# Two neighbouring rows per partition for the gate and up weights of a mixture of experts

## The chip, the cores and the metric

The kernel runs on one core of one Trainium2 chip. The metric is device time in microseconds (us): from the start to the end of one execution, as the median of several runs. The profile shows one execution. Its engines are TensorE (PE for products, PEld for the weight loads into it), VectorE (DVE), ScalarE (ACT), GpSimd (POOL) and SyncE (SP), which mostly issues DMA transfers; sixteen DMA engines move the data between the memory of the chip and the core's SBUF.

## The reference

One layer of a diffusion backbone, for 256 latent and 256 context tokens of 2048 channels, all in float32. A modulated RMS norm feeds one input projection; a state-space branch and a gated short convolution follow, one output projection joins them, and a gated residual is added. Then comes the part that matters here: a second modulated norm, a router, and 16 experts that each choose their 32 best tokens.

```python
mod_lat = jnp.einsum('bd,de->be', jax.nn.silu(c), w_mod[layer]) + b_mod[layer]
sh1_l, sc1_l, g1_l, sh2_l, sc2_l, g2_l = jnp.split(mod_lat[:, None, :], N_MOD, axis=-1)
...
f_lat = modulate(rmsnorm(h_lat, norm_ffn_w[layer]), sh2_l, sc2_l)
aff = jax.nn.softmax(jnp.einsum('bnd,de->bne', h, w_router).astype(jnp.float32), axis=-1)
gates, idx = lax.top_k(jnp.swapaxes(aff, 1, 2), cap)
xe = jax.vmap(lambda hb, ib: hb[ib])(h, idx)
hid = jax.nn.silu(jnp.einsum('becd,edf->becf', xe, w_gate)) * jnp.einsum('becd,edf->becf', xe, w_up)
ye = jnp.einsum('becf,efd->becd', hid, w_down) * gates[..., None].astype(h.dtype)
```

`modulate(h, shift, scale)` is `h * (1 + scale) + shift`. For each expert w_gate and w_up are 2048 x 1024 and w_down is 1024 x 2048, so an expert's three matrices are 8 MiB each and all experts together 384 MiB. The sum over the channels `d` in the products with w_gate, w_up and w_router doesn't depend on the order in which the channels are taken, as long as both factors take them in the same order.

## The kernel before

Channels lie on the 128 partitions. A vector of 2048 channels is a tile of 128 partitions by 16 columns, and column k holds channels 128k to 128k+127; a matrix with 2048 rows is used in 16 tiles of 128 rows in the same way.

**Stages.** First the modulation for the input (`make_mods`, `mod_both`), in chunks of the channels, together with the first blocks of the input projection. Then the rest of the input projection (`gemm`, `gemm_part`), whose weights are loaded by `split_tile` on SP as `raw`, rounded on ScalarE (`whi`, line 89) and reduced to the remainder on VectorE (`wlo`, line 90); the state-space groups and the short convolution work on its results. The later modulation (shift sh2 and scale sc2 of the experts' input, gates g1 and g2) is spread between these blocks: `mod_lat` (lines 221 to 238) loads w_mod by GpSimd as `mraw` into two buffers, sums it on VectorE into `macc` (lines 230 and 232), and at the end of 512 columns transposes `macc` on TensorE (line 236) and reduces it (lines 237 and 238). There are 16 such chunks, four each for sh2, sc2, g1, g2. In the output projection they are loaded one row tile at a time (kn=1, 16 loads to a chunk), before that two at a time.

**Output projection and router.** `h`, the residual stream, lies with tokens on the partitions. As its columns are ready, it is transposed on TensorE (line 765), copied as `hT`, and multiplied with the router's weights `gwr`, which were loaded by SP (line 715) and scaled with G = (1 + sc2) * norm_ffn_w on VectorE (line 719). The top 32 tokens of each expert are found on VectorE; one-hot matrices `oh` follow.

**Experts.** A loop over the 16 experts (from line 877). Line 883 gathers an expert's tokens: 8 products of `oh` with 512 columns of `h` each, recorded as 16. Line 889 transposes them, and line 896 applies G and sh2, giving `xe` with channels on the partitions. Then, for each pair of row tiles k0, k0+1, line 914 loads one tile of w_gate and one of w_up, 1 MiB each, and line 920 multiplies `xe` with them:

```python
nc.sync.dma_start(t.rearrange("p (a b) -> p a b", a=2),
                  w[e_].rearrange("(k p) f -> p k f", p=P)[:, k0:k0 + 2, :])
```

Partition p so receives row 128 k0 + p and row 128 (k0+1) + p, two runs of 4 KB that lie 512 KB apart in memory. After the activation, line 940 loads w_down in 8 tiles of 128 rows, 1 MiB each, where partition p receives one row of 8 KB, and line 943 multiplies. The last expert's w_down is loaded column by column (line 961).

**What sets the order.** A scheduler places the instructions of each engine by their dependences and priorities; the kernel's text gives the priorities. Each engine, and each DMA queue, then takes its instructions in that order. Expert weights go through a ring of 8 KB slots (`wtile`): a slot is loaded again when the products that read it are done. The first slots become free during the output projection, so the first expert's weights are loaded ahead.

**Small parameters.** Before line 182 the rows of c, c_ctx, b_mod, the convolution and norm weights are loaded as r1, r2, r3 and transposed; `bcol` holds b_mod and `nffn` norm_ffn_w as columns. `late_cols` (line 181) does the same for a few that are needed later. GpSimd issues two of the loads (lines 120 and 101), then makes the index pattern `it` (line 125), from which `ident` is made on VectorE (line 127).

## Time and profile before

| what | us |
|---|---|
| three runs | 2017.79, 2019.6, 2024.4 |
| median | 2019.6 |
| span of the profiled execution, from the first to the last instruction | 2012.6 |

The page gives no time of its own for the profiled execution beyond that span; the median of the runs stands 7.0 us above it. Read the page in this order: the span and the chain that ended last (which engines and transfers set the end), then the busy time of the engines by stage, then the stage with the largest share of the chain, instruction by instruction. A busy share over 1 for DMA means that the times of neighbouring packets overlap a little. The profiled time has five parts: up to 20 us the start, to 870 us the input projection and its two branches, to 1010 us the output projection, to 1061 us its end and the router, and from there the experts.

### The profile page before, as it was taken

What the parts mean: (1) busy time and instruction counts of PE and PEld (TensorE: products, weight loads), DVE (VectorE), ACT (ScalarE), POOL (GpSimd) and SP (SyncE); (2) the same over time, 40 slices, a digit from 0 to 9 for tenths busy, and PEclk for the clock granted to TensorE, in tenths of its full rate; (3) what the DMA queues carried; (4) which work ended last, traced back from release to release, by engine and by line L of the source; (5) the groups of instructions that cost most, each with busy time, mean ns of one, the idle gap of its engine ahead of it and who ended that gap; (6) DMA issues with size and microseconds to landing.
All of it is one profiled execution on the core that took longest, in us unless ns stands there. A gap on an engine that the chain in (4) does not pass through costs nothing.

```text
span 2012.6 us, 25496 instructions
## 1 busy us (share of the span) xinstructions
PE 1663.9 (83%) x10316; PEld 995.4 (49%) x10316; DVE 906.1 (45%) x1389; ACT 516.4 (26%) x850; POOL 142.1 (7%) x207
## 2 busy tenths in 40 slices
PE   6999999899999999999988776667676677767675
PEld 4677997778798989777862111111111111111122
DVE  2448966778788878777642110111111111111113
ACT  4323656454566334343320000000000000000002
POOL 1001001111111221211200000000000000000000
PEclk9999999999999999999989889998889889898988
DMA  9975653646476989787888999999999999999997
GB/s 336 384 256 171 197 166 97 197 149 219 144 226 200 313 310 306 261 299 258 271 334 354 413 413 413 412 412 412 414 413 414 412 411 414 414 414 413 411 413 278
DMA packets 210774, 641.10 MB, mean 319 GB/s; under 512 B 17493, under 2 KB 50514, under 8 KB 194400
## 3 DMA queue, kind: packets, MB, share of 16 engines
q1 hardware_dynamic: 191248, 570.20, 74.8%
q0 software_dynamic: 19120, 68.22, 10.6%
q8 instruction: 81, 1.33, 0.3%
q10 hardware_dynamic: 288, 1.05, 0.1%
q14 instruction: 37, 0.30, 0.0%
HBM read 637.31 MB, written 2.10 MB: 318 GB/s over the span
## 4 chain that ended last, share of the span: by engine, by line
DMA 54%; PE 32%; DVE 7%; issue 4%; ACT 1%; SPq 1%; POOL 0%; DVEq 0%; ACTq 0%; POOLq 0%
DMA abig<-in_w_up_dram 12%; PE g L312 10%; DMA mraw<-in_w_mod_dram 10%; PE g L315 9%; DMA mwt<-in_w_up_dram 8%; DMA abig<-in_w_down_dram 8%; DMA mwt<-in_w_down_dram 6%; DMA ebig<-in_w_up_dram 6%; DMA raw<-in_w_in_dram 2%; DVE macc L232 2%; PE gu L920 2%; DVE wlo L90 2%; PE py L613 2%; PE g L747 1%; PE yd L943 1%
## 5 line engine op out<-in xcount | busy, mean ns | idle before, releaser
L315 PE MATMUL g<-abig,whi 128*128 128x256 f32 x2048 | 382.8, 289 | 16.2 <-DVE cvt L377 9.5
L89 ACT CAST whi<-raw 128x1024 fp32r<-128x1024 f32 x241 | 253.7, 1054 | 382.6 <-DMA raw<-in_w_in_dram 101.3
L90 DVE TENSOR_TENSOR wlo<-raw,whi 128x1024 fp32r<-128x1024 f32 x241 | 298.0, 1239 | 100.4 <-ACT whi L89 100.2
L315 PEld LDWEIGHTS g<-abig,whi 128*128 128x128 f32 x2048 | 325.3, 196 | 21.2 <-issue 15.5
L315 PE MATMUL g<-abig,wlo 128*128 128x256 f32 x1024 | 289.2, 289 | 2.0 <-DVE wlo L90 2.0
L920 PE MATMUL gu<-abig,xe 128*32 128x512 f32 x1088 | 205.6, 632 | 85.0 <-DMA abig<-in_w_up_dram 61.0
L232 DVE SCALAR_TENSOR_TENSOR macc<-mraw,csl,macc 128x512 f32<-128x512 f32 x240 | 187.0, 779 | 76.5 <-DMA mraw<-in_w_mod_dram 74.5
L925 DVE SCALAR_TENSOR_TENSOR hid<-hid,gu 64x512 f32<-64x512 f32 x16 | 10.9, 680 | 466.2 <-ACT hid L924 466.2
L312 PE MATMUL g<-abig,whi 128*128 128x512 f32 (+1 forms) x672 | 214.6, 398 | 2.7 <-ACT abig L296 2.5
L924 ACT ACTIVATE hid<-gu 64x512 f32<-64x512 f32 x16 | 9.5, 591 | 781.6 <-PE gu L920 781.6
L315 PEld LDWEIGHTS g<-abig,wlo 128*128 128x128 f32 x1024 | 197.6, 196 | 5.4 <-DVE wlo L90 3.4
L920 PE MATMUL gu<-mwt,xe 128*32 128x512 f32 x616 | 126.9, 660 | 52.0 <-DMA mwt<-in_w_up_dram 39.2
L747 PE MATMUL g<-whi,abig 128*128 128x512 f32 (+1 forms) x640 | 158.5, 351 | 1.9 <-ACT whi L89 1.6
L226 POOL DMA_DIRECT2D mraw<-in_w_mod_dram x152 | 101.3, 667 | 798.0 <-DVE macc L232 569.6
L920 PEld LDWEIGHTS gu<-abig,xe 128*32 128x32 f32 x1088 | 38.7, 111 | 238.0 <-DMA abig<-in_w_up_dram 108.6
L312 PEld LDWEIGHTS g<-abig,whi 128*128 128x128 f32 (+1 forms) x672 | 122.1, 185 | 44.2 <-issue 10.3
L312 PE MATMUL g<-abig,wlo 128*128 128x512 f32 (+1 forms) x336 | 130.5, 393 | 0.0
L747 PEld LDWEIGHTS g<-whi,abig 128*128 128x128 f32 x640 | 112.7, 191 | 17.7 <-ACT whi L89 2.0
L747 PE MATMUL g<-wlo,abig 128*128 128x512 f32 (+1 forms) x320 | 103.1, 354 | 9.1 <-DVE wlo L90 9.0
L954 DVE TENSOR_TENSOR ebig<-ebig,g 128x512 f32<-128x512 f32 x112 | 71.5, 684 | 80.0 <-PE g L950 80.0
L920 PE MATMUL gu<-ebig,xe 128*32 128x512 f32 x344 | 79.3, 699 | 30.1 <-DMA ebig<-in_w_up_dram 21.1
L943 PE MATMUL yd<-abig,hidT 128*32 128x512 f32 x512 | 71.6, 655 | 34.3 <-DMA abig<-in_w_down_dram 30.1
(311 smaller groups left out, 1561.6 us busy)
## 6 DMA issues: line engine op xcount, KB each, us to landing
raw<-in_w_in_dram SPq DMA_DIRECT2D x177, 512.0 KB, 4.6
abig<-in_w_up_dram SPq DMA_DIRECT2D x68, 1024.0 KB, 18.6
abig<-in_w_gate_dram SPq DMA_DIRECT2D x68, 1024.0 KB, 18.8
abig<-in_w_down_dram SPq DMA_DIRECT2D x64, 1024.0 KB, 20.0
mraw<-in_w_mod_dram POOLq DMA_DIRECT2D x104, 512.0 KB, 4.8
mwt<-in_w_down_dram SPq DMA_DIRECT2D x43, 1024.0 KB, 19.9
mwt<-in_w_gate_dram SPq DMA_DIRECT2D x39, 1024.0 KB, 20.0
mwt<-in_w_up_dram SPq DMA_DIRECT2D x38, 1024.0 KB, 18.6
```

The costliest lines, as they stand in the source:

```text
L89: nc.scalar.copy(hv, wv)
L90: nc.vector.tensor_tensor(lv, wv, hv.bitcast(F32), op=OP.subtract)
L226: nc.gpsimd.dma_start(w, w_mod.rearrange("(k p) c -> p k c", p=P)[:, k0:k0 + kn, c0:c0 + 512])
L232: nc.vector.scalar_tensor_tensor(acc, w[:, j], cs, acc, op0=OP.mult, op1=OP.add)
L312: nc.tensor.matmul(banks[ct][0:ncol], st, a[q][:, kk], start=beg, stop=end)
L315: nc.tensor.matmul(banks[ct // 2][0:ncol, o:o + L], st, a[q][:, kk, L:2 * L], start=beg and ct % 2 == 0, stop=end, skip_group_check=True)
L613: nc.tensor.matmul(oo, l, r, start=(i == 0), stop=(i == 3), skip_group_check=True)
L747: nc.tensor.matmul(ob[nn * t + m], yy[i][:, kk, P * t:P * t + P], w[:, j, n * m:n * m + n], start=(kt == order[0] and pi == 0), stop=(kt = ...
L920: nc.tensor.matmul(gu[32 * q:32 * q + 32], xe[:, k], wt[q // 2][:, 1024 * kk + 512 * (q % 2):1024 * kk + 512 * (q % 2) + 512], start=(k == ...
L925: nc.vector.scalar_tensor_tensor(hid, hid, 1.0, gu[0:64], op0=OP.add, op1=OP.mult)
L943: nc.tensor.matmul(yd[32 * q:32 * q + 32], hidT[:, j, 32 * c2:32 * c2 + 32], t[:, 512 * q:512 * q + 512], start=(kt == 0), stop=(kt == FF ...
L954: nc.vector.tensor_tensor(av, h[:, t, 512 * q:512 * q + 512] if e_ == 0 else av, pc[q], op=OP.add)
```

## The change

Two neighbouring rows of w_gate or w_up now go to one partition: partition p of pair b receives rows 256 b + 2p and 256 b + 2p + 1. One tile still holds the same 256 rows, 1 MiB. Row tile k = 2b + i therefore holds channels 256 b + 2p + i, and everything that meets these weights along the channels is paired in the same way:

- the gather of an expert's tokens and the transposes of `h` read every second column of `h`, first the even ones of 256, then the odd ones;
- sh2 and sc2 are transposed out of `macc` with a step of two (`paired`); g1 and g2 are not;
- norm_ffn_w and the parts of b_mod for sh2 and sc2 are loaded once more as `r4` (24 rows of 256, by GpSimd, at the very start), transposed with a step of two in `late_cols`, and kept as `pcol`;
- the router's weights are loaded in two transfers instead of one.

The products' and transposes' numbers and sizes stay. The diff also drops comments, which is left out here; line numbers shift by up to 20.

```diff
+    r4 = pp.tile([24, 256], F32, name="r4")
+    nc.gpsimd.dma_start(r4[0:8], norm_ffn_w[0].rearrange("(k p) -> k p", p=256))
+    nc.gpsimd.dma_start(r4[8:24], b_mod[0, 3 * D:5 * D].rearrange("(k p) -> k p", p=256))
...
+    pcol = const.tile([P, 3, KT], F32, name="pcol")
+    nffn = pcol[:, 0]
...
     def late_cols():
+        pt = sbank("pt")
+        for i in range(2):
+            nc.tensor.transpose(pt[:, 24 * i:24 * i + 24], r4.rearrange("p (c i) -> p i c", i=2)[:, i], ident[0:24, 0:24])
+        nc.vector.tensor_copy(pcol.rearrange("p a (b i) -> p i (a b)", i=2),
+                              pt[:, 0:48].rearrange("p (i c) -> p i c", i=2))
...
-    def mod_lat(c0, dst, pool, kn):
+    def mod_lat(c0, dst, pool, kn, bias, paired):
...
+            av = acc.rearrange("p (b c i) -> p b i c", b=2, i=2)
             for j in range(4):
-                nc.tensor.transpose(pc[:, P * j:P * j + P], acc[:, P * j:P * j + P], ident)
+                src = av[:, j // 2, j % 2] if paired else acc[:, P * j:P * j + P]
+                nc.tensor.transpose(pc[:, P * j:P * j + P], src, ident)
...
-            nc.vector.tensor_tensor(dst, dst, bcol[:, c0 // P:c0 // P + 4], op=OP.add)
+            nc.vector.tensor_tensor(dst, dst, bias, op=OP.add)
...
-            mod_lat((3, 4, 2, 5)[j] * D + 512 * q, dst, pool or mp, kn)
+            c0 = (3, 4, 2, 5)[j] * D + 512 * q
+            bias = pcol[:, 1 + j, 4 * q:4 * q + 4] if j < 2 else bcol[:, c0 // P:c0 // P + 4]
+            mod_lat(c0, dst, pool or mp, kn, bias, j < 2)
...
-    nc.sync.dma_start(wr, w_router.rearrange("(k p) e -> p k e", p=P))
+    for i in range(2):
+        nc.sync.dma_start(wr.rearrange("p (b i) e -> p i b e", i=2)[:, i],
+                          w_router.rearrange("(b p i) e -> p i b e", p=P, i=2)[:, i])
...
-                    nc.tensor.transpose(pt[:, o:o + P], h[:, t, P * (k + kk):P * (k + kk) + P], ident)
+                    hv = h[:, t, P * k:P * k + 2 * P].rearrange("p (c i) -> p i c", i=2)[:, kk]
+                    nc.tensor.transpose(pt[:, o:o + P], hv, ident)
...
+                    hv = h[:, t, 512 * q:512 * q + 512].rearrange("p (b c i) -> p b i c", b=2, i=2)
                     nc.tensor.matmul(pt[32 * q:32 * q + 32], oh[:, t, CAP * e_:CAP * e_ + CAP],
-                                     h[:, t, 512 * q:512 * q + 512], start=(t == 0), stop=(t == 1), skip_group_check=True)
+                                     hv, start=(t == 0), stop=(t == 1), skip_group_check=True)
...
-                                  w[e_].rearrange("(k p) f -> p k f", p=P)[:, k0:k0 + 2, :])
+                                  w[e_].rearrange("(b p i) f -> p b i f", p=P, i=2)[:, k0 // 2])
```

The change moves instructions too, since the scheduler places everything anew. Three places matter. The first is SP at the end of the first expert's loads; `mwt`, `ebig` and `abig` are the slots of the ring, and the sizes are those of the destination. Before:

```order
L914 DMA mwt<-in_w_up_dram 128x2x1024
L940 DMA mwt<-in_w_down_dram 128x2048 x5
L940 DMA ebig<-in_w_down_dram 128x2048 x3
L914 DMA abig<-in_w_gate_dram 128x2x1024
L914 DMA abig<-in_w_up_dram 128x2x1024
```

After:

```order
L934 DMA mwt<-in_w_up_dram 128x2048
L960 DMA mwt<-in_w_down_dram 128x2048 x5
L960 DMA ebig<-in_w_down_dram 128x2048 x3
L934 DMA abig<-in_w_gate_dram 128x2048
L934 DMA abig<-in_w_up_dram 128x2048
```

Nothing moved here; the loads of gate and up have the same form as those of w_down, one run per partition. From the router on, the order of SP is otherwise the same.

The second place is GpSimd at the start of the program (`r_70` is r1, `r_76` is r4). Before:

```order
L1019 UNCONDITIONAL_BRANCH
L120 DMA r_70<-in_ssm_conv_w_dram 72x128
L101 DMA r_70<-in_ssm_conv_b_dram 24x128
L125 ISA
L125 IOTA it 128x128
```

After:

```order
L1039 UNCONDITIONAL_BRANCH
L108 DMA r_76<-in_norm_ffn_w_dram 8x256
L109 DMA r_76<-in_b_mod_dram 16x256
L124 DMA r_70<-in_ssm_conv_w_dram 72x128
L101 DMA r_70<-in_ssm_conv_b_dram 24x128
L129 ISA
L129 IOTA it 128x128
```

Two loads now stand ahead of the index pattern.

The third place is VectorE at the start of the output projection, between the norms of the branches and the router's weights; `macc` is a step of the later modulation, here of its 14th chunk, whose first step reads `macc` from nothing. Before:

```order
L230 TENSOR_SCALAR macc_8145<-mraw_8146,csl_129 128x512
L636 TENSOR_TENSOR abig_8071<-ysc0_1717,abig_8070 128x1024
L636 TENSOR_TENSOR abig_8071<-ebig_5517,abig_8070 128x1024
L636 TENSOR_TENSOR abig_8077<-ebig_6359,abig_8076 128x1024
L232 SCALAR_TENSOR_TENSOR macc_8145<-mraw_8149,csl_129,macc_8145 128x512
L636 TENSOR_TENSOR abig_8077<-ebig_6359,abig_8076 128x1024
L90 TENSOR_TENSOR wlo_8662<-raw_8659,whi_8661 128x1024
L90 TENSOR_TENSOR wlo_8680<-raw_8677,whi_8679 128x1024
L719 TENSOR_TENSOR gwr_8117<-gwr_8117,mods_2482 128x16x16
L721 COPY srow_8138<-psb_8120 1x16
```

After:

```order
L242 TENSOR_SCALAR macc_8154<-mraw_8155,csl_132 128x512
L652 TENSOR_TENSOR abig_8079<-ysc0_1725,abig_8078 128x1024
L652 TENSOR_TENSOR abig_8079<-ebig_5525,abig_8078 128x1024
L652 TENSOR_TENSOR abig_8085<-ebig_6367,abig_8084 128x1024
L244 SCALAR_TENSOR_TENSOR macc_8154<-mraw_8158,csl_132,macc_8154 128x512
L652 TENSOR_TENSOR abig_8085<-ebig_6367,abig_8084 128x1024
L90 TENSOR_TENSOR wlo_8671<-raw_8668,whi_8670 128x1024
L244 SCALAR_TENSOR_TENSOR macc_8154<-mraw_8161,csl_132,macc_8154 128x512
L90 TENSOR_TENSOR wlo_8689<-raw_8686,whi_8688 128x1024
L737 TENSOR_TENSOR gwr_8125<-gwr_8125,mods_2490 128x16x16
L739 COPY srow_8147<-psb_8129 1x16
```

One more step of the modulation stands ahead of the router's weights, between the two remainders of w_out.

## Rows read from the trace of the kernel before

**Rows 1.** The page: span, all DMA packets, and the chain that ended last by engine.

```profile
span 2012.6 us, 25496 instructions
...
DMA packets 210774, 641.10 MB, mean 319 GB/s; under 512 B 17493, under 2 KB 50514, under 8 KB 194400
...
DMA 54%; PE 32%; DVE 7%; issue 4%; ACT 1%; SPq 1%; POOL 0%; DVEq 0%; ACTq 0%; POOLq 0%
```

**Rows 2.** By stage: stretch, length, busy us (instructions) by engine, granted clock, DMA share, GB/s.

```profile
20.00:330.00 310.00, 306.15 (x2103) 246.32 (x2099) 195.55 (x318) 140.80 (x222) 9.91 (x15) 1.00 0.71 233
330.00:870.00 540.00, 512.07 (x3392) 448.43 (x3391) 430.76 (x565) 263.52 (x445) 97.14 (x121) 0.98 0.70 230
870.00:1010.00 140.00, 130.24 (x704) 110.41 (x704) 100.02 (x131) 53.05 (x61) 25.36 (x48) 0.96 0.81 272
...
1061.00:1975.00 914.00, 644.42 (x3636) 141.75 (x3638) 133.97 (x242) 25.59 (x49) 0.58 (x1) 0.90 1.02 410
```

**Rows 3.** Timeline of TensorE, gate and up products: start us, length us, operation, idle before.

```profile
1882.94 1.05 PE L920 MATMUL gu<-mwt,xe 128*32 128x512 f32 x4 [0.65 <-DMA mwt<-in_w_gate_dram]
...
1911.07 1.91 PE L920 MATMUL gu<-abig,xe 128*32 128x512 f32 x12 [1.49 <-DMA abig<-in_w_up_dram]
```

**Rows 4.** The same view, products with w_down, in two experts.

```profile
1191.11 1.07 PE L943 MATMUL yd<-abig,hidT 128*32 128x512 f32 x8 [1.21 <-DMA abig<-in_w_down_dram]
...
1196.12 1.94 PE L943 MATMUL yd<-abig,hidT 128*32 128x512 f32 x8 [1.44 <-DMA abig<-in_w_down_dram]
...
1309.45 1.07 PE L943 MATMUL yd<-mwt,hidT 128*32 128x512 f32 x8 [1.20 <-DMA mwt<-in_w_down_dram]
...
1319.40 1.06 PE L943 MATMUL yd<-abig,hidT 128*32 128x512 f32 x8 [0.81 <-DMA abig<-in_w_down_dram]
```

**Rows 5.** Columns as in rows 2: gate and up alone, then w_down alone.

```profile
1140.00:1175.00 35.00, 26.14 (x124) 5.01 (x120) 4.51 (x8) 0.00 (x0) 0.00 (x0) 0.89 1.03 411
1177.00:1195.00 18.00, 12.29 (x88) 3.13 (x82) 2.80 (x6) 1.55 (x3) 0.00 (x0) 0.91 1.01 419
```

**Rows 6.** The same view around the first expert, and over the full stream.

```profile
1056.00:1066.00 10.00, 8.16 (x71) 3.11 (x75) 3.52 (x11) 0.59 (x1) 0.35 (x1) 1.00 0.36 125
1066.00:1076.00 10.00, 9.19 (x88) 2.60 (x80) 0.10 (x1) 0.59 (x1) 0.00 (x0) 1.00 1.01 416
...
1096.00:1960.00 864.00, 604.06 (x3338) 130.27 (x3332) 125.31 (x226) 24.04 (x46) 0.58 (x1) 0.90 1.02 413
```

**Rows 7.** The gather, then TensorE's transposes of h and macc: ns min/median/max.

```profile
1056.78 1.92 PE L883 MATMUL pt<-h,oh 128*32 128x512 f32 x16
...
L765 PEld LDWEIGHTS pt<-ident,h x32: 137/141/223, 1013.4 to 1037.9; 128*128 128x128 f32 x32
L765 PE MATMUL pt<-ident,h x32: 272/273/328, 1013.5 to 1038.0; 128*128 128x128 f32 x32
...
L236 PEld LDWEIGHTS pc<-ident,macc x64: 137/141/231, 338.7 to 1013.3; 128*128 128x128 f32 x64
```

**Rows 8.** Timeline of the program's first 20 us.

```profile
2.02 0.54 POOL L101 DMA_DIRECT2D r<-in_ssm_conv_b_dram  x1
2.64 0.28 POOL L125 IOTA it<- 128x128 f32 x1
...
3.99 0.31 PE L153 MATMUL pt<-ident,r 32*128 32x32 f32 x1 [3.99 <-DVE ident L127]
...
10.64 0.29 DVE L254 TENSOR_SCALAR diag<-ident,rs 128x128 f32<-128x128 f32 x1 [0.76 <-POOL rs L249]
```

**Rows 9.** The router's weights: their load, its landing, and the first products.

```profile
869.54 0.38 SPq L715 DMA_DIRECT2D gwr<-in_w_router_dram  x1
...
DMA to landing us min/median/max: 6.2/6.2/6.2
...
L718 PE MATMUL psb<-gwr,mods x32: 176/176/177, 883.3 to 884.1; 128*1 128x16 f32 x32
```

**Rows 10.** The later modulation's loads in the output projection: ns min/median/max, first and last start.

```profile
L226 POOL DMA_DIRECT2D mraw<-in_w_mod_dram x48: 536/538/592, 869.5 to 1008.8; - x48
```

More of the change, by code (lines that the diff above doesn't have):

```diff
@@ L174, in layer @@
     scw = col2[:, 0:48].rearrange("p (t k) -> p t k", t=3)
-    nmix, nffn, nssm, nsc = (col2[:, 48 + 16 * i:64 + 16 * i] for i in range(4))
+    nmix, _, nssm, nsc = (col2[:, 48 + 16 * i:64 + 16 * i] for i in range(4))
+    pcol = const.tile([P, 3, KT], F32, name="pcol")
+    nffn = pcol[:, 0]
     cw = col1[:, 0:72].rearrange("p (t k) -> p t k", t=3)
```

## The prediction

> **What bounds the kernel now.** I read the page's head and chain first, then the busy time by stage, then the stage that carries the chain. The span is 2012.6 us, and the chain that ended last is 54% DMA and 32% TensorE [rows 1]. The stage table splits that [rows 2]: from 20 to 870 us TensorE is busy 306.15 of 310 and 512.07 of 540 us, from 870 to 1010 us 130.24 of 140; this front is TensorE's. From 1061 to 1975 us it is busy only 644.42 of 914 us while the DMA share is 1.02. The experts wait for their weights.
>
> The rate inside that stage can be read without any packet rows, because TensorE starts on each transfer as it lands. With gate and up loads in flight its starts lie between 1882.94 and 1911.07 us, 12 starts and so 11 intervals: 28.13 / 11 = 2.557 us for each 1 MiB transfer [rows 3]. With w_down in flight four intervals run from 1309.45 to 1319.40 us (2.488 each) and two from 1191.11 to 1196.12 us (2.505 each) [rows 4]; I take the middle, 2.496 us. Both kinds move the same 1 MiB to the same 128 partitions. What differs is the piece: gate and up come in 4 KB runs, two to a partition, w_down in one 8 KB run. The windows that hold one kind alone agree: 411 GB/s for gate and up, 419 for w_down [rows 5]. The stream is not full before the first expert starts: at 1056 to 1066 us the share is 0.36, at 1066 to 1076 us it is 1.01, and it stays at 1.02 to 1960 us [rows 6]. It restarts when expert 0's products free slots.
>
> **Gate and up, the gain.** The order shows that each of these loads becomes 128x2048, the form in which w_down already stands; nothing is added to it. I therefore price it at w_down's 2.496 us: 2.557 - 2.496 = 0.061 us less for each. Expert 0's 16 loads are issued before the stream fills, and TensorE is busy 9.19 of the 10 us after 1066 us [rows 6] with products that don't wait for them, so they gain nothing at the end. Experts 1 to 15 have 15 x 16 = 240 loads in the full stream: 240 x 0.061 = 14.6 us. The bounds: 1 MiB at 411 and 419 GB/s is 2.551 and 2.503 us, 0.048 apart, 11.5 us; with the fastest w_down interval, 2.488, it is 0.069 and 16.6 us. I take 14.6, since the intervals count transfers and a window also holds its edges. TensorE does not become late: 604.06 us busy of 864 [rows 6], 70%. Next late is the same as now, the stream, then the last expert's column-wise w_down loads, which the change leaves alone.
>
> The same per piece: 1 MiB in half as many pieces lands 0.061 us sooner [rows 3, 4]; each of the 16 DMA engines has 128 / 16 = 8 pieces fewer per load, so the trace's price is 0.061 / 8 = 7.6 ns a piece. [...]
>
> **Token gather, residual transposes, modulation transposes.** The instruction counts stay; the operand read from SBUF now steps over every second float. In the 16 products that gather an expert's tokens it is the moving operand: 1.92 us in all for expert 0 [rows 7], on the path, because the experts' stream cannot restart before them; for the other 15 experts they lie beside the stream. In the 32 transposes of h it is the weight load, 141 ns median under products of 273 ns [rows 7], on the approach to the router, where TensorE is on the path. In 32 of the 64 transposes of the later modulation (the shift and scale of the experts' input) it is again the weight load, 141 ns [rows 7], in the front that TensorE bounds. No row shows such a step on TensorE. The lower bound is nothing, since as many elements are read; a gain is excluded, because nothing is left out. The upper bound is half rate: 1.92 + 32 x 0.141 + 32 x 0.141 = 10.9 us. The nearest rows, the same instructions on packed operands, say nothing of a step; I take 0, the price of the nearest rows, and leave 10.9 to a rival.
>
> [...]
>
> **Start.** Two loads of r4 stand ahead of the index pattern on GpSimd. A load there takes 0.54 us [rows 8], so the pattern, now at 2.64 us, comes about 1.1 us later, and so does ident, which is made from it and released the first product at 3.99 us. Who needs ident on the path is the diagonal at 10.64 us, and what it waited for last was the statistics of ctx from GpSimd [rows 8], not ident: over 6 us of cover. The transposes of c and b_mod at 3.99 us slide by the same 1.1 us, and their results are first needed after that diagonal. Cost 0; without the cover 1.1 us.
>
> **late_cols.** Two transposes and one VectorE copy are added. By the 0.31 us of a similar 32-row product [rows 8] I put 0.4 us on TensorE, which is full there: +0.4 us. The r4 loads have long landed, so the wait that is added costs nothing, and queued behind it are the transposes of r1 and the first products of C.
>
> **Router weights.** One load becomes two, both on SP. The one before took 0.38 us to issue at 869.54 us and 6.2 us to land [rows 9]; a second one lands by about 877 us, and its first reader starts at 883.3 us. Cost 0; behind it on SP stands one w_out load, 0.4 us later.
>
> **The moved order.** The scheduler has interleaved all engines anew up to the router. The work is the same, so what can change is TensorE's idle time: 3.85 + 27.93 + 9.76 = 41.5 us from 20 to 1010 us [rows 2]. A gain cannot exceed that; a loss has no bound from the trace, only a likely size. Where the order shows the output projection, the last modulation chunks stand 3 steps in instead of 2 when the router weights are scaled, which is level. I take 0 and give it 6 us to either side, an estimate: a seventh of that idle time.
>
> **Sum.** -14.6 + 0.4 = -14.2 us on this execution's 2012.6 us span, so 1998.4 us. The median of the runs, 2019.6 us, is 7.0 us above the span, for what lies around it; I leave those 7.0 us as they are: 2005.4 us. From 14.2 -/+ (11.5 to 16.6 for the loads, 6 for the order) and about 2 us between runs I put the forecast's own range at 1997 to 2014 us.
>
> **Rivals.** (a) *The step over every second float halves TensorE's reading*: 2005.4 + 10.9 = 2016.3 us, no difference that can be told. For it: no row shows the step. Against it: the instructions read as many elements as before, and a weight load is partly covered by the product ahead of it. 10%. (b) *The packet is not the price*: gate and up stay at 2.557 us because w_down is faster for another reason, such as what stands beside it. Then only 0.4 us is left, 2020.0 us. For it: w_down comes in one stretch of eight per expert. Against it: both rates change at every border between the kinds and hold inside it [rows 3 to 5]. That the change doesn't do what it says belongs here, and the order speaks against it. 4%. (c) *Slower: the late modulation slips.* In the output projection 48 single loads of w_mod are issued between 869.5 and 1008.8 us [rows 10], one per 139.3 / 47 = 2.96 us, each waiting for the VectorE step that frees its buffer, and VectorE's in-order queue holds the remainders of w_out (wlo) behind steps whose load has not landed. If the new order carried one chunk of 16 steps more into that stage, it would cost 16 x 2.96 = 47 us: 2005.4 + 47 = 2052 us. It decides from (14.2 + 6) / 2.96 = 7 steps on. Against it: the order, which is one step ahead there. 4%. (d) *Only half of w_down's lead belongs to the piece*, the other half to its place in the stream, so that gate and up land every 2.527 us: 7.3 us saved, 2005.4 + 7.3 = 2012.7 us, inside the forecast's range. For it: the windows already give only 0.048 [rows 5]. Against it: the interval is the same at the middle of w_down's stretch as at its end [rows 4]. 7%. [...]
>
> **How the numbers follow.** A measurement of this kernel can tell about 0.3%, 6.1 us, from no change, so faster is below 2013.5 us. The forecast has 75%, of it 0.73 faster and 0.02 the same; (d) gives 0.05 and 0.02; (a) 0.02 faster, where the step costs only part of its price, and 0.08 the same; (b) 0.04 the same; (c) 0.04 slower. Together faster 0.80, same 0.16, slower 0.04. The range that should hold 8 in 10 takes the forecast's own range, (d), and the low edge of what (a) can partly give: 1997 to 2015 us.
>
> **What would show it.** Right: the starts of the gate and up products 2.50 us apart; about 32768 packets fewer in the page's 210774 [rows 1]; the rate of the full stretch near 418 GB/s instead of 413; the experts' stage 14 to 15 us shorter, its start within 6 us of 1061 us. The transposes of h at 273 ns and their weight loads at 141 ns; more there is (a). Starts 2.56 us apart are (b). Idle time before the remainders of w_out, and a first expert product after 1075 us, are (c). The forecast is wrong most easily through the start of that first product: each microsecond there moves the end by one.

## The result

| what | before, us | after, us |
|---|---|---|
| median of six runs each | 2017.07 | 2002.84 (1996.63 to 2007.26) |
| span of the profiled execution | 2012.6 [rows 1] | 1994.8 |

The ratio of the two is 0.9926, 95% interval 0.9902 to 0.9949: 14.2 us less at the medians. The changed kernel was run again later beside the kernel before, and came to 2003.75 us against 2015.67 us, ratio 0.9941 (0.9924 to 0.9958). The forecast was 2005.4 us in a range from 1997 to 2015.

The page of the changed kernel, the lines that answer to [rows 1]: the span, all DMA packets, and the chain that ended last by engine.

```profile
span 1994.8 us, 25507 instructions
...
DMA packets 178086, 641.12 MB, mean 321 GB/s; under 512 B 17549, under 2 KB 50594, under 8 KB 128944
...
DMA 58%; PE 22%; issue 9%; DVE 8%; ACT 1%; SPq 1%; POOL 1%; DVEq 0%; POOLq 0%; ACTq 0%
```

There are 32688 packets fewer than before, and the count under 2 KB is up by 80. So 65536 packets of 4 KB became 32768 of 8 KB, as many as the change joins, and 80 small ones came, 56 of them under 512 B. The bytes are the same to 0.02 MB. The chain is more DMA than before, not less: it takes another way through the front, with less of TensorE in it, while the end is still set by the experts' weights.

The stages of the changed kernel, columns as in [rows 2]; the last four lines answer to [rows 5, 6].

```profile
20.00:330.00 310.00, 307.36 (x2111) 246.94 (x2112) 199.74 (x324) 144.85 (x236) 9.88 (x15) 1.00 0.70 231
330.00:870.00 540.00, 510.08 (x3382) 445.57 (x3381) 420.83 (x561) 259.48 (x431) 97.18 (x120) 0.98 0.71 230
870.00:1010.00 140.00, 131.28 (x727) 112.09 (x727) 102.34 (x134) 54.39 (x66) 26.15 (x49) 0.98 0.84 280
...
1066.00:1076.00 10.00, 7.32 (x71) 2.14 (x60) 1.37 (x2) 0.96 (x2) 0.00 (x0) 1.00 1.00 419
1096.00:1942.00 846.00, 591.64 (x3296) 128.62 (x3292) 125.04 (x224) 24.01 (x46) 0.58 (x1) 0.91 1.01 420
1140.00:1175.00 35.00, 23.48 (x130) 4.51 (x130) 3.49 (x6) 0.59 (x1) 0.00 (x0) 1.00 1.01 419
1177.00:1195.00 18.00, 12.97 (x92) 3.32 (x92) 2.11 (x5) 0.59 (x1) 0.00 (x0) 0.88 1.01 420
```

The front is the same within 2 us of TensorE's busy time in each stage. In the full stretch the rate is 420 GB/s where it was 413, with the DMA share at 1.01, before 1.02 [rows 6], so the engines were full before and after; they move more in the same busy time. The window that held gate and up alone at 411 GB/s and the one that held w_down alone at 419 [rows 5] now show 419 and 420: the two kinds have become one.

TensorE's timeline shows the same by transfer. Gate and up products of the changed kernel, columns as in [rows 3]:

```profile
1869.41 1.91 PE L940 MATMUL gu<-mwt,xe 128*32 128x512 f32 x12 [1.44 <-DMA mwt<-in_w_up_dram]
1871.91 1.05 PE L940 MATMUL gu<-mwt,xe 128*32 128x512 f32 x4 [0.60 <-DMA mwt<-in_w_gate_dram]
...
1894.32 1.91 PE L940 MATMUL gu<-abig,xe 128*32 128x512 f32 x12 [1.44 <-DMA abig<-in_w_up_dram]
```

From the first to the last of these, ten intervals, it is 24.91 us, 2.491 us for each; before it was 2.557 [rows 3].

Where the 17.8 us between the two spans went is read from the first product and the last product that waited for an up load. Before, then after:

```profile
1061.25 2.34 PE L920 MATMUL gu<-ebig,xe 128*32 128x512 f32 x18 [1.18 <-DVE xe L896]
...
1974.43 1.91 PE L920 MATMUL gu<-abig,xe 128*32 128x512 f32 x12 [1.51 <-DMA abig<-in_w_up_dram]
```

```profile
1058.94 2.34 PE L940 MATMUL gu<-ebig,xe 128*32 128x512 f32 x18 [1.18 <-DVE xe L916]
...
1956.68 1.91 PE L940 MATMUL gu<-abig,xe 128*32 128x512 f32 x12 [1.50 <-DMA abig<-in_w_up_dram]
```

Between them lie 913.2 us before and 897.7 us after: 15.4 us came from the experts' stream, 2.3 us from an earlier start, and the tail is the same. How much of the 2.3 us belongs to the change is a question for the experiments.

### The profile page after: what moved, and what is told of

Read it like the earlier page. It is cut to its first block, busy times and chain, and to the rows that moved or that the text cites. A ratio compares the mean times of both kernels' runs of the same rounds, so it can differ in the third digit from the quotient of the medians.

```text
span 1994.8 us, 25507 instructions
## 1 busy us (share of the span) xinstructions
PE 1651.4 (83%) x10318; PEld 991.2 (50%) x10318; DVE 900.3 (45%) x1390; ACT 516.6 (26%) x850; POOL 143.9 (7%) x209
## 4 chain that ended last, share of the span: by engine, by line
DMA 58%; PE 22%; issue 9%; DVE 8%; ACT 1%; SPq 1%; POOL 1%; DVEq 0%; POOLq 0%; ACTq 0%
DMA abig<-in_w_up_dram 16%; DMA mwt<-in_w_up_dram 9%; PE g L329 9%; DMA mraw<-in_w_mod_dram 9%; DMA abig<-in_w_down_dram 8%; PE g L326 6%; DMA mwt<-in_w_down_dram 6%; DMA ebig<-in_w_up_dram 5%; DVE macc L244 3%; DVE wlo L90 2%; DMA raw<-in_w_in_dram 2%; DMA ebig<-in_w_down_dram 1%; DMA raw<-in_w_out_dram 1%; PE pm L216 1%; PE s L329 1%
## 5 line engine op out<-in xcount | busy, mean ns | idle before, releaser
L329 PE MATMUL g<-abig,whi 128*128 128x256 f32 x2048 | 376.3, 287 | 15.2 <-ACT whi L89 7.5
L89 ACT CAST whi<-raw 128x1024 fp32r<-128x1024 f32 x241 | 253.9, 1054 | 381.7 <-DMA raw<-in_w_in_dram 92.5
L90 DVE TENSOR_TENSOR wlo<-raw,whi 128x1024 fp32r<-128x1024 f32 x241 | 293.6, 1221 | 102.7 <-ACT whi L89 100.2
L329 PEld LDWEIGHTS g<-abig,whi 128*128 128x128 f32 x2048 | 319.8, 194 | 21.3 <-issue 11.8
L945 DVE SCALAR_TENSOR_TENSOR hid<-hid,gu 64x512 f32<-64x512 f32 x16 | 10.9, 679 | 444.9 <-ACT hid L944 444.9
L940 PE MATMUL gu<-mwt,xe 128*32 128x512 f32 x616 | 122.5, 629 | 49.9 <-DMA mwt<-in_w_up_dram 37.1
L940 PE MATMUL gu<-ebig,xe 128*32 128x512 f32 x344 | 73.4, 636 | 28.5 <-DMA ebig<-in_w_up_dram 18.9
```

Source lines behind the costliest of these rows:

```text
L89: nc.scalar.copy(hv, wv)
L90: nc.vector.tensor_tensor(lv, wv, hv.bitcast(F32), op=OP.subtract)
L329: nc.tensor.matmul(banks[ct // 2][0:ncol, o:o + L], st, a[q][:, kk, L:2 * L], start=beg and ct % 2 == 0, stop=end, skip_group_check=True)
L940: nc.tensor.matmul(gu[32 * q:32 * q + 32], xe[:, k], wt[q // 2][:, 1024 * kk + 512 * (q % 2):1024 * kk + 512 * (q % 2) + 512], start=(k == ...
L945: nc.vector.scalar_tensor_tensor(hid, hid, 1.0, gu[0:64], op0=OP.add, op1=OP.mult)
```

## The experiments

One table for all kernels that keep the sizes of the transfers at 1 MiB. A transfer lands when the last of its data has arrived. "Gate, up" and "w_down" are the time from one landing to the next, as the mean over an expert's stretch of one kind, and of these the median over the experts; "stream" is the time from the first to the last of the 352 landings of experts 1 to 15, up to the last up load; all are worked out from the landings in each kernel's trace. "Start" is the first gate product of expert 0.

| kernel | gate, up us | w_down us | stream us | start us | time us | ratio to before |
|---|---|---|---|---|---|---|
| before | 2.557 | 2.496 | 897.5 | 1061.25 | 2017.07 | |
| after | 2.493 | 2.493 | 882.0 | 1058.94 | 2002.84 | 0.9926 (0.9902 to 0.9949) |
| after_again | 2.492 | 2.493 | 882.0 | 1064.57 | 2003.75 | 0.9941 (0.9924 to 0.9958) |
| b_8k | 2.492 | 2.493 | 881.8 | 1063.10 | 2001.81 | 0.9920 (0.9895 to 0.9945) |
| a_4k | 2.557 | 2.495 | 897.7 | 1060.67 | 2018.12 | 1.0014 (0.9997 to 1.0031) |
| a_down4k | 2.497 | 2.557 | 890.0 | 1064.58 | 2013.37 | 0.9990 (0.9971 to 1.0009) |
| a_2k | 2.706 | 2.499 | 933.3 | 1061.86 | 2053.04, one run | |
| a_packed | 2.492 | 2.493 | 882.0 | 1061.35 | 2000.86, one run | |
| a_step4 | 2.492 | 2.493 | 882.0 | 1061.63 | 1999.27, one run | |

The theory was that the number of pieces per transfer sets the rate of the stream and that all else in the change is worth about nothing. Its rivals were that w_down leads for another reason (its place in the stream), that the moved order has a share in the gain, and that the strided reads on TensorE cost time.

**The load alone: b_8k.** The kernel before, with nothing but the new view of the two weights; the order of the instructions is the same on every engine.

```diff
-                                  w[e_].rearrange("(k p) f -> p k f", p=P)[:, k0:k0 + 2, :])
+                                  w[e_].rearrange("(b p i) f -> p b i f", p=P, i=2)[:, k0 // 2])
```

> The kernel before with one edit: gate and up are loaded with two neighbouring rows per partition, nothing else is paired (so the products over the channels meet the wrong weights; the work is the same). All engines keep the order of before, SP's loads alone change form. Theory (the piece is the price): 2.557 to 2.493 us per gate and up load, 240 loads, 15 us faster than before, and nothing else moves: first gate product at about 1061 us as before. Rival (the re-ordered front gave part of the gain): clearly less than 15 us here.

It gave 2001.81 us against 2015.96 us, 14.2 us less, which is the whole gain of the change. Its window over 800 us of the stream, columns as in [rows 2], has the rate of the changed kernel:

```profile
1100.00:1900.00 800.00, 566.04 (x3096) 121.00 (x3092) 115.82 (x208) 20.15 (x39) 0.00 (x0) 0.90 1.01 420
```

So neither the moved order nor the paired channels are needed for the gain, and what they cost is too small to stand out here.

**The change without the load: a_4k.** The line above put back in the changed kernel.

> The changed kernel with one edit undone: gate and up are loaded as before, 4 KB per row, while everything else stays paired (the products meet the wrong weights). Theory: gate and up land every 2.557 us again, the experts' part is as long as in the kernel before, and the time against before is the price of everything else in the change: the steps over every second float, the added loads and the new order, between -3 and +3 us. Rival (the pairing and the order brought some of the gain): 4 us or more faster than before.

2018.12 us, ratio 1.0014: no difference to the kernel before that can be told, and the stream is back at 897.7 us. With b_8k this closes the question from both sides: with the load alone all of the gain, without it none.

**w_down in 4 KB pieces: a_down4k.** The changed kernel, where a tile of w_down now takes half rows of two row tiles, so that w_down has the pieces that gate and up had.

```diff
-                nc.sync.dma_start(t, w_down[e_, P * kt:P * kt + P, :])
+                r0, h0 = 2 * P * (kt // 2), 1024 * (kt % 2)
+                nc.sync.dma_start(t.rearrange("p (a b) -> p a b", a=2),
+                                  w_down[e_, r0:r0 + 2 * P, h0:h0 + 1024].rearrange("(a p) f -> p a f", p=P))
```

> The changed kernel, but w_down is loaded in 4 KB pieces: each load takes half rows of two row tiles (the product meets the wrong weights). Theory: the number of pieces sets the rate wherever it is, so w_down lands every 2.557 us while gate and up stay at 2.493; 15 x 8 = 120 loads x 0.064 = 7.7 us slower than the changed kernel. Rival (w_down was faster because of its place in the stream or of what is beside it): w_down stays at 2.49, no slower.

The two kinds change places: w_down lands every 2.557 us, gate and up every 2.497 us. TensorE's timeline of a_down4k, products with w_down, then with gate and up (eight intervals between the last two lines, 19.97 / 8 = 2.496 us):

```profile
1257.35 1.06 PE L965 MATMUL yd<-mwt,hidT 128*32 128x512 f32 x8 [1.50 <-DMA mwt<-in_w_down_dram]
1259.91 1.06 PE L965 MATMUL yd<-mwt,hidT 128*32 128x512 f32 x8 [1.50 <-DMA mwt<-in_w_down_dram]
...
1282.53 1.91 PE L940 MATMUL gu<-abig,xe 128*32 128x512 f32 x12 [1.45 <-DMA abig<-in_w_up_dram]
...
1302.50 3.58 PE L940 MATMUL gu<-mwt,xe 128*32 128x512 f32 x12 [1.47 <-DMA mwt<-in_w_up_dram]
```

The lead went with the piece and left the place in the stream, which refutes rivals (b) and (d). It isn't the distance in memory either: a partition's two runs lie 512 KB apart in a_4k and 1 MB apart here, and both forms land every 2.557 us. The stream grew by 8.0 us; 14 x 8 = 112 loads at 0.065 us are 7.3 us, and the other 0.7 us is not explained.

**2 KB pieces: a_2k.** The same for gate and up with four pieces of 2 KB to a partition.

```diff
-                nc.sync.dma_start(t.rearrange("p (a b) -> p a b", a=2),
-                                  w[e_].rearrange("(b p i) f -> p b i f", p=P, i=2)[:, k0 // 2])
+                r0, h0 = 4 * P * (k0 // 4), 512 * (k0 // 2 % 2)
+                nc.sync.dma_start(t.rearrange("p (a b) -> p a b", a=4),
+                                  w[e_, r0:r0 + 4 * P, h0:h0 + 512].rearrange("(a p) f -> p a f", p=P))
```

> The changed kernel with gate and up in 2 KB pieces: each load takes a quarter of the columns of four row tiles (the products meet the wrong weights). Theory (a fixed price per piece, 7.6 to 8 ns on each of 16 engines): 32 pieces per engine and load in place of 16 at 4 KB add 16 x 7.8 ns = 0.125 us, so 2.68 us per load, 240 x 0.187 = 45 us slower than the changed kernel. Rival (what counts is that a partition's bytes are in one run, whatever the size): like the 4 KB form, 2.56 us and 15 us slower.

2.706 us for each transfer, a little over the theory's 2.68, and a stream of 933.3 us. The windows of a_4k, a_down4k and a_2k over the same 800 us show the rates; the last number of a line is GB/s, the one before it the DMA share.

```profile
1100.00:1900.00 800.00, 562.77 (x3058) 119.64 (x3052) 116.11 (x208) 20.12 (x39) 0.00 (x0) 0.89 1.02 413
```

```profile
1100.00:1900.00 800.00, 562.68 (x3110) 119.52 (x3104) 118.51 (x213) 20.15 (x39) 0.00 (x0) 0.90 1.02 416
```

```profile
1100.00:1900.00 800.00, 545.62 (x2960) 115.58 (x2956) 109.79 (x199) 20.11 (x39) 0.00 (x0) 0.89 1.04 397
```

The share is full in all three; only the rate differs. Each of the 16 engines has 8 pieces of a transfer at 8 KB, 16 at 4 KB, 32 at 2 KB. From 8 to 4 KB a piece costs (2.557 - 2.4925) / 8 = 8.1 ns, from 4 to 2 KB (2.706 - 2.557) / 16 = 9.3 ns. The packets' own times in the traces, from 1200 to 1900 us, show the same: 88, 164, 315 and 618 ns on average at 2, 4, 8 and 16 KB (a_2k, a_4k, after, and a_16k_b below). Two packets take 11 to 13 ns more than one of twice the size, at every size; that is more than the landings give, as the times of neighbouring packets overlap a little (a DMA share of 1.01 to 1.04).

**What the strided reads cost: a_packed and a_step4.** In a_packed the changed kernel's three kinds of read go back to packed operands; in a_step4 the gather, and all 64 transposes of the later modulation, read every fourth float. The three places in a_packed, and the two in a_step4:

```diff
-                src = av[:, j // 2, j % 2] if paired else acc[:, P * j:P * j + P]
+                src = acc[:, P * j:P * j + P]
...
-                    hv = h[:, t, P * k:P * k + 2 * P].rearrange("p (c i) -> p i c", i=2)[:, kk]
+                    hv = h[:, t, P * (k + kk):P * (k + kk) + P]
...
-                    hv = h[:, t, 512 * q:512 * q + 512].rearrange("p (b c i) -> p b i c", b=2, i=2)
+                    hv = h[:, t, 512 * q:512 * q + 512]
```

```diff
-            av = acc.rearrange("p (b c i) -> p b i c", b=2, i=2)
+            av = acc.rearrange("p (c i) -> p i c", i=4)
...
-                    hv = h[:, t, 512 * q:512 * q + 512].rearrange("p (b c i) -> p b i c", b=2, i=2)
+                    hv = h[:, t, 512 * q:512 * q + 512].rearrange("p (c i) -> p i c", i=4)
```

> The changed kernel, but TensorE reads packed columns again in the transposes of h, in the gather of the tokens and in the modulation transposes (so the channels of the experts' input no longer match the paired weights). Same order on every engine. Theory (the step over every second float is a small price on TensorE): the weight loads of the transposes of h fall from 209 to 141 ns median and four transposes from 0.68 to 0.59 us on the path; the gather's products from 612 to 592 ns at full clock; together 1 to 3 us less up to the first gate product, nothing in the experts. Rival (the longer weight loads come from the new order, not from the step): they stay at 209 ns.

> The changed kernel, but the gather and all 64 modulation transposes read every fourth float instead of every second (other channels are paired, so the output is not the reference's); the transposes of h stay at every second. [...] Rival (any step costs the same): 209 and 612 ns.

The transposes of h (L784) and of the modulation (L250) and the gather (L903), ns min/median/max: first the changed kernel, then a_packed, then a_step4.

```profile
L784 PEld LDWEIGHTS pt<-ident,h x32: 195/209/261, 1011.1 to 1036.1; 128*128 128x128 f32 x32
L784 PE MATMUL pt<-ident,h x32: 280/283/386, 1011.3 to 1036.3; 128*128 128x128 f32 x32
...
L903 PE MATMUL pt<-h,oh x256: 609/1054/1061, 1053.2 to 1902.9; 128*32 128x512 f32 x128
```

```profile
L784 PEld LDWEIGHTS pt<-ident,h x32: 138/141/225, 1013.9 to 1038.3; 128*128 128x128 f32 x32
L784 PE MATMUL pt<-ident,h x32: 272/273/333, 1014.0 to 1038.4; 128*128 128x128 f32 x32
...
L903 PE MATMUL pt<-h,oh x256: 592/600/1061, 1055.7 to 1907.2; 128*32 128x512 f32 x128
```

```profile
L250 PEld LDWEIGHTS pc<-ident,macc x64: 195/210/370, 339.9 to 1012.9; 128*128 128x128 f32 x64
...
L903 PE MATMUL pt<-h,oh x256: 1059/1080/1089, 1055.3 to 1905.7; 128*32 128x512 f32 x128
```

A weight load of 128 x 128 goes from 141 to 209 ns by the step of two, and stays at 210 ns by a step of four, as the rival of a_step4 had it. The moving operand does otherwise. The gather's medians mix two levels of the clock in the first two kernels (16 products of the changed kernel take 1.98 us from 1082.94 us, at a granted clock of 1.00, and 3.64 us from 1780.11 us, at 0.50), so I compare the least, 592 ns packed and 609 ns by two; by four the median is 1080 ns, and at a granted clock of 1.00 (expert 0's gather, 3.79 us) a product takes about as long as the packed read at 0.50 (1061 ns, its greatest). The time of the two kernels lies inside the spread of the changed kernel, as a difference of a microsecond or two has to in single runs. The 1 to 3 us that a_packed was to start its experts earlier cannot be told for the same reason: its start, 1061.35 us, is one of a range of starts that one program alone spans (below).

**Larger pieces for w_down: a_16k and a_16k_b.** If a piece costs 8 ns, 16 KB pieces halve their number once more: 4 pieces fewer per MiB and engine, 0.032 us. In a_16k w_down of experts 0 to 14 comes as 2 MiB, two neighbouring rows to a partition, in three slots of its own; the intermediate `hid` is transposed in the paired order.

```diff
...
-                t = wtile()
-                nc.sync.dma_start(t, w_down[e_, P * kt:P * kt + P, :])
+                if kt % 2 == 0:
+                    wd = mw.tile([P, 2, 2048], F32, name="mwt", tag="mwt")
+                    nc.sync.dma_start(wd, w_down[e_, P * kt:P * kt + 2 * P, :].rearrange("(p i) f -> p i f", i=2))
+                t = wd[:, kt % 2]
```

> The changed kernel carried on: the first 15 experts' w_down is loaded as 2 MiB with two neighbouring rows, 16 KB, per partition, into 3 slots of 16 KB that take the place of 6 of 8 KB; the transposes of the hidden values are paired to match; gate and up have 13 slots. Theory (about 8 ns per piece and engine): 2 MiB land in 2 x 2.493 - 0.064 = 4.92 us, 60 loads save 3.8 us against the changed kernel, some 19 us against the kernel before. Rivals: a piece over 8 KB is not cheaper (4.99 us, same as the changed kernel); or the fewer slots let the stream run dry (slower than the changed kernel, with a DMA share under 1 in the experts).

It gave 2007.64 us, ratio 0.995 (0.9931 to 0.9969): faster than the kernel before, no gain over the change. The piece did what it should: a 2 MiB load lands 4.92 us after the transfer ahead of it, the median of 50 such loads. The stream lost it again at its start. In a_16k's windows, columns as in [rows 2]:

```profile
1061.00:1100.00 39.00, 28.76 (x204) 8.07 (x203) 4.61 (x11) 1.55 (x3) 0.00 (x0) 0.76 0.83 340
...
1120.00:1140.00 20.00, 17.45 (x128) 4.25 (x128) 0.72 (x2) 0.59 (x1) 0.00 (x0) 0.84 0.87 351
...
1400.00:1900.00 500.00, 348.19 (x1946) 86.71 (x1942) 73.55 (x135) 12.38 (x24) 0.00 (x0) 0.86 1.01 422
```

The full stretch runs at 422 GB/s, but 1061 to 1100 and 1120 to 1140 us don't. The first of these is no loss of a_16k's own. In after_again (the changed kernel once more, below), which has no such slots, the same window shows less still, since the stream restarts there with the first expert:

```profile
1061.00:1100.00 39.00, 34.74 (x250) 10.58 (x250) 8.31 (x18) 2.13 (x4) 0.00 (x0) 0.84 0.80 327
```

The second is a break, for after_again has 422 GB/s from 1120 to 1140 us. SP's timeline of a_16k shows what went before it. Four w_down loads, the fourth of expert 0 and three of expert 1, hold the queue for 20.63 us while they wait for the three slots, and the gate tile that expert 1's first product reads is issued behind them:

```profile
1086.75 20.63 SPq L964 DMA_DIRECT2D mwt<-in_w_down_dram  x4
1107.43 0.42 SPq L934 DMA_DIRECT2D ebig<-in_w_gate_dram  x1
```

a_16k_b loads expert 0's last two row tiles through the common ring, which removes the wait of expert 0's fourth load; the ring's order was fitted to it. Its theory reads the 340 GB/s from 1061 to 1100 us as the loss, which the line of after_again contradicts. It was measured beside after_again. The edit against a_16k:

```diff
-    ring = [ebig] * 3 + [abig] * 10
+    ring = [ebig] + [abig] * 2 + [ebig] * 2 + [abig] * 8
...
+                if e_ == 0 and kt >= FF // P - 2:
+                    wd = wtile().rearrange("p (a b) -> p a b", a=1)
+                    nc.sync.dma_start(wd[:, 0], w_down[0, FF - 2 * P:FF, :].rearrange("(p i) f -> p i f", i=2)[:, kt % 2])
...
```

> The changed kernel with w_down of experts 0 to 14 loaded as 2 MiB, 16 KB per partition, in three slots of their own, as in a_16k; the one difference to a_16k is that the last two row tiles of expert 0's w_down come as two 1 MiB loads through the common ring, so that no load waits for a 16 KB slot before the experts start. Theory (a_16k lost its gain only because that load, held on SP, held expert 1's gate and up loads behind it, 340 GB/s from 1061 to 1100 us): the DMA share from 1066 us is about 1.0 again as in the changed kernel, a 2 MiB load lands in 4.90 us instead of 4.985, 56 such loads of experts 1 to 14 save 56 x 0.08 = 4.5 us, and the time is about 2002.8 - 4.5 = 1998.3 us, some 0.2% below the changed kernel of the same call. Rival (three 16 KB slots are too few in every expert, because a slot comes free only after both of its row tiles are multiplied): the share stays below that of the changed kernel at the borders between experts too, the gain is used up, and the time is 2003 to 2008 us, level with or above the changed kernel.

> The changed kernel again, beside a_16k_b on the same chip, so that the two can be compared at a few us. Theory and rival alike: about 2003 us, ratio 0.993 to the kernel before. What it tells besides is how far two executions of one program differ in the front: my theory is that the first gate product starts within 3 us of the 1058.94 us of the first profile, and that the gate and up loads land 2.49 us apart again; if the intervals differed between two executions as much as between the two kernels (0.06 us), the price per piece would be noise.

a_16k_b came to 2006.57 us (2002.03 to 2011.48), ratio 0.9958 (0.9944 to 0.9971), and after_again to 2003.75 us: 2.8 us more with intervals that overlap, and not the 1998.3 us that the theory gave. Three lines of a_16k_b on TensorE. The last two show the transfer: from the start on a gate load to that on the 2 MiB behind it 4.90 us (4.92 by the landings, the median of 50), where two of 1 MiB take 2 x 2.493 = 4.99.

```profile
1118.55 1.92 PE L940 MATMUL gu<-ebig,xe 128*32 128x512 f32 x4 [25.30 <-DMA ebig<-in_w_gate_dram]
...
1285.28 1.05 PE L940 MATMUL gu<-abig,xe 128*32 128x512 f32 x4 [0.58 <-DMA abig<-in_w_gate_dram]
1290.18 3.24 PE L971 MATMUL yd<-mwt,hidT 128*32 128x512 f32 x16 [3.86 <-DMA mwt<-in_w_down_dram]
```

The first is a wait of expert 1's first product: 25.30 us for a gate load. SP's timeline of a_16k_b tells why:

```profile
1081.63 3.76 SPq L967 DMA_DIRECT2D mwt<-in_w_down_dram  x3
...
1096.24 0.33 SPq L934 DMA_DIRECT2D ebig<-in_w_gate_dram  x1
1122.68 0.33 SPq L934 DMA_DIRECT2D ebig<-in_w_up_dram  x1
```

With slots of its own, expert 1's w_down was free to load early, and three loads, 3 x 4.9 = 14.7 us of the stream, went ahead of five gate and up loads, among them the gate tile that expert 1's first product reads. TensorE stood without it, no slot came free, and SP issued nothing from 1096.57 to 1122.68 us. The stream broke for it, where it had broken in a_16k too:

```profile
1120.00:1140.00 20.00, 16.79 (x138) 4.71 (x140) 1.37 (x2) 0.96 (x2) 0.00 (x0) 0.93 0.89 358
...
1400.00:1900.00 500.00, 355.47 (x1938) 89.98 (x1934) 74.78 (x136) 12.38 (x24) 0.00 (x0) 0.83 1.01 422
```

358 GB/s for 20 us is a loss of 62 x 20 / 420 = 3.0 us, against a gain of at most 4.5 us over the rest. What the landings show is 880.2 us from the first gate load of expert 1 to the last up load, 1.8 us less than in the changed kernel. These 1.8 us are lost in the tail: from the last up load's landing to the end it takes 41.3 us, and 38.2 in the changed kernel. Expert 14's last 2 MiB and the products that read them stand ahead of expert 15's last gate and up products on TensorE:

```profile
1951.40 3.44 PE L971 MATMUL yd<-mwt,hidT 128*32 128x512 f32 x16 [3.88 <-DMA mwt<-in_w_down_dram]
...
1963.68 1.05 PE L940 MATMUL gu<-abig,xe 128*32 128x512 f32 x4
```

These end 5.8 us after the last up load has landed (1964.7 and 1958.9 us), in the changed kernel 2.0 us after it (1958.6 and 1956.6). The time lies in the rival's range, 2003 to 2008 us, but not for the rival's reason: later borders show no loss, 422 GB/s over 500 us against 420 in after_again. What else lies between the profile of a_16k_b and its median, 4.5 us above that run, stays open. The version that was worth keeping is the change itself.

## Why the prediction was right

**The gain.** The step that carried the forecast, gate and up at w_down's rate because they now have its piece, held. Its term was 14.6 us and measured 15.5 us (897.5 to 882.0): the landings give 2.4925 and not 2.496 us for the 8 KB transfer, 0.0649 us each, 240 x 0.0649 = 15.6. The windows' lower bound of 11.5 us was too low: at 2.557 and 2.496 us 1 MiB moves at 410.1 and 420.1 GB/s, where the two windows showed 411 and 419; that this is due to their edges, as the prediction said, is likely but not shown. The upper bound of 16.6 held.

**The price of a piece.** The prediction's 7.6 ns measured 8.1 ns here, 9.3 ns between 4 and 2 KB, and between 8 and 16 KB (4.985 - 4.92) / 8 = 8 ns by the landings, 10.6 ns by the 4.90 us of the two starts above.

**Strided reads.** Taken as 0, bounded by 10.9 us; that step was wrong in kind and nearly right in size. By the prediction's own sign, h transposes over 273 ns and weight loads over 141 ns, rival (a) has set in, but at a tenth of its price. The weight load of the transposes is 68 ns longer, 48%. But it lies beside the product ahead (from 1019.82 us four weight loads take 0.56 us, and their four products 0.74 us from 1019.83), and the product is longer by 10 ns only at the median, by 58 ns in the longest case (386 against 328 ns). The chain that ended last shows what is left on the path: one batch of four transposes of h, before and then after, us of start and length.

```profile
1021.98 0.59 PE pt L765 x4
```

```profile
1019.89 0.68 PE pt L784 x4
```

Over the 32 transposes of h the chain has 4.16 us before and 4.73 after, 0.57 us more. The 32 strided transposes of the modulation at the same price are another 0.57 us; a gather at a granted clock of 1.00 goes from 1.90 to 1.98 us. Together about 1.2 us, an estimate from one execution of each. So the sign of rival (a) came and its price did not: no read took twice as long (+48% and +3%), and most of what it took longer lies under the cover that the prediction had named against it.

**The front.** Start, router weights and late_cols were priced at 0 and 0.4 us, and the trace of the changed kernel bears that out. The index pattern and the first product (5.01 us, before 3.99) come 1.0 us later, but the diagonal does not [rows 8]; in after_again it starts at 10.96 us, so it moves by some tenths between executions. The two transposes of late_cols take 0.41 us:

```profile
3.66 0.26 POOL L129 IOTA it<- 128x128 f32 x1
...
10.39 0.29 DVE L268 TENSOR_SCALAR diag<-ident,rs 128x128 f32<-128x128 f32 x1 [0.76 <-POOL rs L263]
...
54.12 0.41 PE L191 MATMUL pt<-ident,r 24*128 24x24 f32 x2
```

The router's two loads are issued at 870.4 and 870.8 us and land 5.4 us later; their first reader starts at 884.0 us. The moved order was 0 with 6 us to either side. The measure for that is after_again: the same program started its first gate product at 1064.57 us and not at 1058.94, with the stream at 882.0 us in both. I had expected the two within 3 us; they are 5.6 apart, and 5.4 of that stands before the first transpose of h (1011.3 and 1016.6 us). So the 2.3 us of the first profile can't be put down to the change, and the other starts in the table, from 1060.67 to 1064.58 us, tell no order from another. What can be said is the balance: 15.5 us from the stream, 14.2 and 11.9 us at the medians of the two series, so some 1 to 4 us were given back or are spread between runs; the 0.4 + 1.2 us above are a part of it, and the rest isn't settled. That the first series gives just the 14.2 us of the sum is in part luck: the stream gained 0.9 us more than its term, and the reads, priced at 0, took about as much.

**The sum.** It took the 7.0 us between span and median for what lies around the span. That was wrong: in each run that has both, time and span are 1.7 to 1.9 us apart (1996.63 and 1994.8 in the first of after), so the profiled execution of before took about 2014.4 us, some 5 us below the median. It did no harm, since the difference was added to both sides. The forecast's 2005.4 us lies 2.6 us above the result, and 2.5 of that is the base: it was the median of three runs, 2019.6 us, and six give 2017.07.

**Rival (c)**, the late modulation slipping by steps, did not occur: 49 single loads of w_mod against 48, and the start of the experts within 6 us of 1061 in all executions.

## What to carry to other kernels

Where a stream of weights sets the time and its share is full, compare the landing interval of its kinds of transfer: equal bytes at unequal intervals, here 2.557 and 2.496 us, showed the price of a piece, and multiplied by the number of transfers in the full stream they gave the stream's gain here within a microsecond, though the pieces were already 4 KB. Joining pieces pays if the reads that it reorders cost less than that (here about 1.2 us), and if it leaves the slots as they are: larger tiles with slots of their own let the scheduler load them ahead of what was needed first. Before reading 2 or 3 us of an earlier start as an effect, run the same program twice.

## What was not expected of the hardware

- A strided read costs a weight load and a moving operand differently. The weight load takes 141 ns packed and 209 to 210 ns with a step of two or four; the moving operand of 512 columns takes at the least 592 ns packed, 609 with a step of two and 1059 with a step of four.
- The price of a piece is nearly the same from 2 to 16 KB, 8 to 11 ns on each DMA engine, so 420 GB/s at 8 KB is not yet the end: 422 GB/s with a third of the bytes in 16 KB pieces.
- The granted clock falls to half around the router and the first expert, at another time in each execution: it was 0.50 from 1040 to 1050 us in the kernel before, from 1054 to 1057 us in the changed kernel and from 1060 to 1066 us in after_again. The first 18 products of expert 0 took 2.34 us in the first profile of the changed kernel and 4.48 us in after_again:

```profile
1064.57 4.48 PE L940 MATMUL gu<-ebig,xe 128*32 128x512 f32 x18 [1.18 <-DVE xe L916]
```

  Its clock there, the third number from the end, was 0.50, after a stretch in which TensorE was busy 3.88 of 6 us:

```profile
1054.00:1060.00 6.00, 3.88 (x25) 1.94 (x27) 5.23 (x19) 0.00 (x0) 0.35 (x1) 1.00 1.02 425
1060.00:1066.00 6.00, 4.65 (x22) 1.61 (x18) 2.03 (x6) 0.59 (x1) 0.00 (x0) 0.50 0.17 68
```

  The gather of expert 0 met the clock of 0.50 in both executions of the changed kernel, 3.21 us in the first profile and 2.71 in after_again, where it was 1.92 before [rows 7]. That is not the price of the strided read: with packed operands a_packed's took 2.71 us as well, at a granted clock of 0.72 from 1054 to 1060 us.
